# Order of the work at chunk borders in a hybrid decoder step: one product chain prioritised, one split cut in two, one weight cast queued later

## The chip, the cores and the metric

One core of a Trainium2 chip runs the whole program. The metric is the device time of one execution in microseconds, as the median of the timed runs. PE is the matrix engine (PEld its weight loads), DVE the vector engine, ACT the scalar engine, POOL the GpSimd engine, SP the engine that only issues DMAs here. Each engine takes its instructions in the order in which they were put into its queue.

## The reference

One inference step of a decoder trunk, in fp32, on 520 tokens (512 of a prompt, 8 of samples): a SwiGLU feed-forward network (FFN), a mixer (causal pooling beside a state-space scan), a second FFN, a final norm.

```python
def _swiglu(x, wg, wu, wd):
    return (jax.nn.silu(x @ wg) * (x @ wu)) @ wd

h = h + 0.5 * _swiglu(_rms_norm(h, ffn1_norm[l]), ffn1_w_gate[l], ffn1_w_up[l], ffn1_w_down[l])
m, p, c, s = _hybrid_mixer(_rms_norm(h, mix_norm[l]), ...)
h = h + m
h = h + 0.5 * _swiglu(_rms_norm(h, ffn2_norm[l]), ffn2_w_gate[l], ffn2_w_up[l], ffn2_w_down[l])
```

The model width is 1024, the hidden width of each FFN 2816, that is 22 tiles of 128. The change touches the two FFNs alone.

## The kernel before

**Precision.** An fp32 product is made of three passes of a faster fp32r product (`mm3`, lines 123, 126, 127): each operand is split into a high part (an ACT cast, line 107 for weights, 268 for activations) and a low part (the difference, a DVE subtraction, lines 114 and 269). For some halves of the weights the low part is made in another way: ACT writes the negated operand (line 110), and a DMA from the POOL queue adds the original weight onto it from memory (line 111).

**Seven products for eight.** The 520 tokens are two halves of 260. A *step* multiplies a 2x2 block of weights with a 2x2 block of activations (two row groups by two halves of tokens) in seven products instead of eight. For that, sums and differences of weight blocks and of activation blocks are formed. For the activations they stand in seven *slots* of 260 columns: slots 0 to 2 are plain blocks, slots 3 to 6 are differences. The products are numbered 1 to 7, and product 1 reads slot 0, 2 reads 1, 3 reads 2, 7 reads 4, 5 reads 3, 6 reads 5, 4 reads 6. In a step they are traced in the order 1, then product 4 of the step before, then 5, 6, 3, 7, 2 (`step`, `product`, `flush`). The results gather in PSUM tiles A and BE. ACT copies partial results out of them to `ac` (line 437); a later product that adds onto the same tile has to wait for that copy.

**Weights of a step.** `load` takes two raw tiles (one buffer `raw`, two of them in turn, loaded by two SP DMAs, line 366), adds them up on DVE (lines 385 to 387) and splits four groups: `a` (products 1 and 2), `c` (products 7 and 5), `d` (products 6 and 3), `b` (product 4). The names in the profile end in these letters: whi_1d_0b is the high part of group b of FFN 1, a down step, chunk 0 (buffer and row numbers are left out). Groups a and b have three buffers together (whi, wlo), c and d two (shi, slo). The last reader of a raw buffer is group b's negated copy.

**Chunks.** The 22 hidden tiles are taken in chunks of 6, 6, 6 and 4. For the first three (`PAIRED`), the gate/up steps (profile names by number, whi_5a) make the hidden activations, and then four down steps multiply them with the down weights (profile names A1d, BE1d, A2d, BE2d for PSUM, digit 1 or 2 for the FFN). Between the last gate/up step of a chunk and its first down step, the first gate/up step of the next chunk is put, so that PE has work while the last hidden tile is finished. The fourth chunk goes another way (`down`, `down_by_half`).

**The chain at a border.** When the products of a hidden tile are done, `gates` runs: DVE adds the copies (line 449), multiplies by the norm's scale (455), ACT applies Silu (456), DVE multiplies again (458) and then with the up part (`up`, 464; half of the tokens here, the other half in `close`, once product 4 is done). For the second tile of each pair `g_split` then forms the slots: DVE makes three differences (272, 273, 274) into `gd`, and `low` casts and subtracts (268, 269) slot 0 (gx), slot 2 and slots 3 to 5 (one instruction of 780 columns); with the second half, a fourth difference (282) and slots 1 and 6. For the last tile of a chunk this is done in two parts in this way; for the others all at once.

**What sets the order.** The program is traced once; a planner with a model of the engines' times then puts each engine's instructions in an order, from what it holds to be ready and from priorities. `tc.high_priority()` raises the priority of what is traced inside it; `tc.issue_after(ins)` puts what is traced inside it, on the engine of `ins`, behind `ins` in that engine's queue, without waiting for its end. In the second FFN each step also carries a small part of the state update of the mixer (`state`), whose ACT and POOL work is kept in its own order.

Of the kernel before, what the change touches and what calls it, by code (L numbers as in the profile page):

```python
# [11 lines left out]
AF = mybir.ActivationFunctionType  # L12
ALU = mybir.AluOpType
# [8 lines left out]
HB = NT // 2  # L22
# [12 lines left out]
PAIRED = 3  # L35
# [26 lines left out]
def tile_trunk_step(ctx: ExitStack, tc: tile.TileContext, ins: dict, outs: dict):  # L62
    nc = tc.nc
# [6 lines left out]
    wp = ctx.enter_context(tc.tile_pool(name="wp", bufs=3, side="right"))  # L70
# [9 lines left out]
    h = vx[:, NVEC:].rearrange("p (d t) -> p d t", d=KD)  # L80
# [10 lines left out]
        hp, nb = (wp, 2) if hp is None else (hp, 1)  # L91
        return hp.tile([P, 2, 1024], F32, tag="raw", bufs=nb, name=f"raw_{name}")

    half = []

    def raw_tile(name):
        if not half:
# [4 lines left out]
    def split(src, n, name, hp, nb, tags, late=None):  # L102
        hi, lo = (hp.tile([P, 1024], F32R, tag=t, bufs=nb, name=f"{t}_{name}")[:, :n] for t in tags)
        h, l = hi, lo
        if len(src.shape) == 3:
            h, l = (t.rearrange("p (j c) -> p j c", j=src.shape[1]) for t in (hi, lo))
        nc.scalar.copy(h, src)  # L107
        q = 0 if late is None else n - late.shape[1]
        if late is not None:
            nc.scalar.activation(out=lo[:, q:], in_=src[:, q:], func=AF.Copy, scale=-1.0)  # L110
            nc.gpsimd.dma_start(out=lo[:, q:], in_=late, accum_op=ALU.add)
        if late is None or q:
            s = slice(0, q) if late is not None else slice(None)
            nc.vector.tensor_tensor(out=l[:, s], in0=src[:, s], in1=h[:, s].bitcast(F32), op=ALU.subtract)
        return hi, lo

    def load_unit(src, n, name, late=False):
        raw = raw_tile(name)[:, :n]
        nc.sync.dma_start(out=raw, in_=src)
        return split(raw, n, name, wp, 3, ("whi", "wlo"), src if late else None)  # L120
# [87 lines left out]
    class Ffn:  # L208
# [42 lines left out]
        def g_split(self, f, late=None):  # L251
            role = self.role(f)
            if role == "plain" and late is not False:
                self.g_plain(f, self.out[f])
            if role != "second":
                return
            last = f == self.chunks[self.chunk[f]][-1]
            if not last and late is False:
                return
            gx, go = self.gx, self.out[f]  # L260
            if not last or late is not True:
                self.gt[f] = (self.gp.tile([P, 14, HB], F32R, tag="gt", bufs=3, name=f"gt{self.i}_{f}"),
                              self.gp.tile([P, 4, HB], F32, tag="xd", name=f"gd{self.i}_{f}"))
            t, xd = self.gt[f]

            def low(x, q):
                hi, lo = t[:, 0:7][:, q], t[:, 7:14][:, q]
                nc.scalar.copy(hi, x)
                nc.vector.tensor_tensor(out=lo, in0=x, in1=hi.bitcast(F32), op=ALU.subtract)

            if not last or late is not True:
                nc.vector.tensor_tensor(out=xd[:, 0], in0=gx[:, 0], in1=gx[:, 1], op=ALU.subtract)
                nc.vector.tensor_tensor(out=xd[:, 1], in0=go[:, 1], in1=gx[:, 1], op=ALU.subtract)
                nc.vector.scalar_tensor_tensor(out=xd[:, 2], in0=xd[:, 1], scalar=-1.0, in1=gx[:, 0], op0=ALU.mult,
                                               op1=ALU.subtract)
                low(gx[:, 0], 0)
                if last:
                    low(go[:, 1], 2)
                    low(xd[:, 0:3], slice(3, 6))
            if last and late is False:  # L280
                return
            nc.vector.scalar_tensor_tensor(out=xd[:, 3], in0=xd[:, 2], scalar=-1.0, in1=go[:, 0], op0=ALU.mult,
                                           op1=ALU.subtract)
            if last:
                low(go[:, 0], 1)
                low(xd[:, 3], 6)
            else:
                low(go, slice(1, 3))
                low(xd, slice(3, 7))
# [101 lines left out]
        def load(self, k):  # L391
            wx = self.wx
            n, src, nb, raw, f1, f2, add = self.added.pop(k) if k in self.added else self.sums(k)
            d1 = split(raw[:, 0, : 2 * nb], 2 * nb, f"{n}a", wp, 3, ("whi", "wlo"), src[0, :, nb:])
            if add is not None:
                add()
            e1 = split(f1, 2 * nb, f"{n}c", wx, 2, ("shi", "slo"))
            e2 = split(f2, 2 * nb, f"{n}d", wx, 2, ("shi", "slo"))
            d2 = split(raw[:, 1, nb : 2 * nb], nb, f"{n}b", wp, 3, ("whi", "wlo"), src[1, :, nb:])
            m = nb // P  # L400
            self.w[k] = {1: (d1, 0), 2: (d1, m), 7: (e1, 0), 5: (e1, m), 6: (e2, 0), 3: (e2, m), 4: (d2, 0)}

# [41 lines left out]
        def gates(self, k):  # L444
            n = f"{self.i}_{k}" if not isinstance(k, tuple) else f"{self.i}d{k[1]}_{k[0]}"
            r = self.nx[3].rearrange("p (b t) -> p b t", b=2)
            tg = self.tg[k] = self.wx.tile([P, 2, HB], F32, tag="tg", bufs=2, name=f"tg{n}")
            a, c = self.ac[k]
            nc.vector.tensor_tensor(out=tg, in0=self.BE[k][:, :, :HB], in1=a, op=ALU.add)  # L449
            if isinstance(k, tuple):  # L450
                hd, hn = h[:, k[1]], h[:, k[1] + 1, HALVES[1]]
                nc.vector.tensor_tensor(out=hd, in0=hd, in1=tg.rearrange("p b t -> p (b t)"), op=ALU.add)
                nc.vector.tensor_tensor(out=hn, in0=hn, in1=c[:, 0], op=ALU.subtract)
                return
            nc.vector.tensor_tensor(out=tg, in0=tg, in1=r, op=ALU.mult)  # L455
            nc.scalar.activation(out=tg, in_=tg, func=AF.Silu)  # L456
            self.g_homes(k)
            nc.vector.tensor_tensor(out=tg, in0=tg, in1=r, op=ALU.mult)  # L458
            self.up(k, 1, c[:, 0])
            self.g_split(k, False)  # L460

        def up(self, k, b, u):
            out, tg = self.out[k][:, b], self.tg[k][:, b]
# [2 lines left out]
        def close(self, k):  # L466
            if isinstance(k, tuple):
                hn = h[:, k[1] + 1, HALVES[0]]
                nc.vector.tensor_tensor(out=hn, in0=hn, in1=self.A[k][:, :HB], op=ALU.subtract)
                return  # L470
            self.up(k, 0, self.A[k][:, :HB])
            self.g_split(k, True)

        def scales(self):
            return rstds(self.nx, f"f{self.i}")
# [823 lines left out]
```

## Time and profile before

| | |
|---|---|
| timed runs | 973.34, 981.19, 981.55 us; median 981.19 us |
| profiled execution | 977.54 us, of which the span from first to last instruction is 975.8 us |
| granted PE clock of the profiled execution | 0.995 |
| instructions on PE, DVE, ACT, POOL | 7636, 1610, 1287, 341 |
| first FFN | to about 357 us of the span |
| mixer | about 357 to 624 us |
| second FFN | from about 602 us to the end |

How to read the rows: an instruction's row gives its start in us from the span's start, its length, the engine, the line of the kernel, the operation, what it writes and reads, the shape, and how many were merged into the row; in square brackets the idle time of its engine before it, and whose end ended that idle time. Rows of groups give busy time, mean ns of one, and idle time before. PE's matmuls overlap each other: one shows 0.28 us, and in a dense stretch the next starts 0.12 us after it. SPq is the queue of SP, in which the loads are issued.

### The profile page before, as it was taken

The page shows a single profiled execution, that of the slowest core. Times are in us where ns is not written, and L with a number is a line of the kernel's source. Part 1 is how long each engine was busy: PE and PEld are TensorE (multiplying, and loading weights), DVE is VectorE, ACT ScalarE, POOL GpSimd, SP SyncE. Part 2 cuts the span into 40 slices and gives each one's busy share as a digit, 9 for nine tenths or more (in the row PEclk, how much of TensorE's full clock was granted, in tenths as well). Part 3 has the DMA queues.
Part 4 walks back from the last instruction along what each step waited for, and adds up shares of the span by engine and source line. Part 5 has one row for each costly group of instructions (what it writes and reads, how often), then busy time and mean ns, then how long its engine had stood idle before and what let it go on. Part 6 is the DMA issues. An engine that isn't in the chain of part 4 may idle for free.

```text
span 975.8 us, 20309 instructions
## 1 busy us (share of the span) xinstructions
PE 945.4 (97%) x7636; PEld 924.0 (95%) x7636; DVE 856.6 (88%) x1610; ACT 700.3 (72%) x1287; POOL 233.6 (24%) x341
## 2 busy tenths in 40 slices
PE   7999999999999999999899999999999999999995
PEld 6999999999999999999799999899999999999995
DVE  7999899989989698688879866999989999999876
ACT  8776777777777475686676546678778788887864
POOL 0111211221121000156522111122332333333300
PEclk9999999999999999999999999999999999999998
DMA  7665766576566243264588777467687678777732
GB/s 242 167 154 136 190 149 148 126 184 180 119 152 165 66 150 118 88 205 117 148 232 225 177 173 165 119 146 179 152 220 185 167 174 222 178 159 189 191 90 89
DMA packets 66739, 157.01 MB, mean 161 GB/s; under 512 B 9608, under 2 KB 22856, under 8 KB 66640
## 3 DMA queue, kind: packets, MB, share of 16 engines
q1 hardware_dynamic: 41168, 103.78, 33.5%
q0 software_dynamic: 25472, 51.92, 29.3%
q8 instruction: 60, 0.98, 0.4%
q14 instruction: 39, 0.32, 0.1%
HBM read 148.33 MB, written 7.34 MB: 160 GB/s over the span
## 4 chain that ended last, share of the span: by engine, by line
PE 81%; DVE 7%; ACT 4%; DMA 4%; issue 2%; POOL 1%; SPq 0%; DVEq 0%; ACTq 0%; POOLq 0%
PE A L127 7%; PE A L123 7%; PE A L126 7%; PE BE L123 6%; PE BE L126 6%; PE BE L127 6%; PE P L315 3%; PE wo L123 2%; PE wo L127 2%; PE wo L126 2%; PE A1d L127 2%; PE A1d L126 2%; PE A1d L123 2%; DMA ab<-scr_acs 1%; PE A2d L127 1%
## 5 line engine op out<-in xcount | busy, mean ns | idle before, releaser
L437 ACT COPY ac<-A 128x260 f32<-128x260 f32 x123 | 45.3, 370 | 20.5 <-PE A L127 20.1
L385 DVE TENSOR_TENSOR s<-raw 128x1024 f32<-128x1024 f32 x41 | 49.9, 1217 | 2.6 <-DMA raw<-in_w2gu 2.4
L1005 POOL DMA_DIRECT2D out_nss<-hs x32 | 20.6, 643 | 84.3 <-DVE hs L1023 74.9
L123 PE MATMUL inz<-xh_mx,whi_inz 128*128 128x260 f32 x128 | 37.5, 293 | 1.0 <-DVE E L1099 1.0
L315 PE MATMUL P<-xg_f,raw 128*128 128x260 f32 x128 | 32.7, 409 | 5.4 <-DMA raw<-in_w1gu 5.4
L123 PE MATMUL wo<-catg,whi_wo 128*128 128x260 f32 x128 | 37.1, 290 | 0.0
L126 PE MATMUL inz<-xl_mx,whi_inz 128*128 128x260 f32 x128 | 36.9, 288 | 0.0
L127 PE MATMUL inz<-xh_mx,wlo_inz 128*128 128x260 f32 x128 | 36.9, 288 | 0.0
L123 PE MATMUL inx<-xh_mx,whi_inx 128*128 128x260 f32 x128 | 36.4, 285 | 0.0
L127 PE MATMUL wo<-catg,wlo_wo 128*128 128x260 f32 x128 | 36.2, 283 | 0.0
L127 PE MATMUL inx<-xh_mx,wlo_inx 128*128 128x260 f32 x128 | 36.2, 283 | 0.0
L126 PE MATMUL wo<-catg,whi_wo 128*128 128x260 f32 x128 | 36.1, 282 | 0.0
L126 PE MATMUL inx<-xl_mx,whi_inx 128*128 128x260 f32 x128 | 36.1, 282 | 0.0
L315 PEld LDWEIGHTS P<-xg_f,raw 128*128 128x128 f32 x128 | 25.7, 205 | 9.5 <-ACT xg_f L192 5.4
L449 DVE TENSOR_TENSOR tg<-BE,ac 128x520 f32<-128x520 f32 x41 | 28.4, 692 | 5.2 <-PE BE L127 5.2
L869 DVE SCALAR_TENSOR_TENSOR A<-U,h,A 128x544 f32<-128x544 f32 x36 | 28.1, 781 | 4.9 <-ACT A L867 4.6
L107 ACT CAST whi_wo<-raw_wo 128x1024 fp32r<-128x1024 f32 x12 | 12.6, 1047 | 27.0 <-issue 18.1
L1123 DVE TENSOR_TENSOR h<-wo,h 128x260 f32<-128x260 f32 x48 | 19.4, 419 | 13.7 <-PE wo L127 13.7
L458 DVE TENSOR_TENSOR tg<-tg,r_f 128x520 f32<-128x520 f32 x41 | 28.4, 693 | 1.2 <-ACT tg L456 1.0
L975 DVE SCALAR_TENSOR_TENSOR junk<-h,cb 128x128 f32<-128x128 f32 x64 | 21.5, 335 | 8.2 <-DMA cb<-scr_bc 7.3
L455 DVE TENSOR_TENSOR tg<-tg,r_f 128x520 f32<-128x520 f32 x41 | 28.4, 692 | 0.1
L386 DVE TENSOR_TENSOR s<-s,raw 128x512 f32<-128x512 f32 x41 | 28.0, 682 | 0.0
(1802 smaller groups left out, 4805.6 us busy)
## 6 DMA issues: line engine op xcount, KB each, us to landing
raw<-in_w2gu SPq DMA_DIRECT2D x44, 512.0 KB, 5.0
raw<-in_w1gu SPq DMA_DIRECT2D x42, 512.0 KB, 4.6
raw_1d<-in_w1d SPq DMA_DIRECT2D x24, 384.0 KB, 3.9
raw_2d<-in_w2d SPq DMA_DIRECT2D x24, 384.0 KB, 4.1
raw_wo<-in_w_out SPq DMA_DIRECT2D x12, 512.0 KB, 6.1
wlo_wo<-in_w_out POOLq DMA_DIRECT2D x12, 512.0 KB, 7.4
ab<-scr_acs SPq DMA_DIRECT2D x8, 512.0 KB, 5.4
h<-in_state_ssm SPq DMA_DIRECT2D x16, 256.0 KB, 6.5
```

The source lines that it names most:

```text
L123: first = nc.tensor.matmul(ps, whi, xhi, start=start, stop=False, **kw)
L126: nc.tensor.matmul(ps, whi, xlo, start=False, stop=False, **kw)
L127: nc.tensor.matmul(ps, wlo, xhi, start=False, stop=stop, **kw)
L315: nc.tensor.matmul(self.banks[f, u][b][:, :HB], ws(self.raw[f][:, u], j + 4 * q), xg[:, slot[q]], start=j == q == 0, stop=j == 3 and q == ...
L385: nc.vector.tensor_tensor(out=s1, in0=diag, in1=up0, op=ALU.add)
L386: nc.vector.tensor_tensor(out=s2[:, 0], in0=s1[:, 1], in1=raw[:, 0, :nb], op=ALU.add)
L437: nc.scalar.copy(keep, out[:, :HB])
L449: nc.vector.tensor_tensor(out=tg, in0=self.BE[k][:, :, :HB], in1=a, op=ALU.add)
L455: nc.vector.tensor_tensor(out=tg, in0=tg, in1=r, op=ALU.mult)
L458: nc.vector.tensor_tensor(out=tg, in0=tg, in1=r, op=ALU.mult)
L869: nc.vector.scalar_tensor_tensor(out=A[:, :n], in0=U[:, j : j + n], scalar=w(j), in1=A[:, :n], op0=ALU.mult, op1=ALU.add)
L975: nc.vector.scalar_tensor_tensor(out=junk, in0=h0[:, q], scalar=1.0, in1=cb, op0=ALU.mult, op1=ALU.mult, accum_out=ysm[:, 4 * g + q, b : b ...
```

## The change

Three things are changed, all in the FFNs.

1. `g_split`: the third difference is computed from the first instead of from the second (the same value), and for the last tile of a chunk slot 3 is split alone, then slots 4 and 5 together, then slot 2; before, slot 2 was split first and then slots 3 to 5 together.
2. `load`: every ACT cast of a weight split is noted, and group b's split (cast and negated copy on ACT) is queued behind the newest one, which is group d's cast. This holds for gate/up and for down steps.
3. `first_if`: for the last tile of each of the three paired chunks, the multiplications, the Silu, the up part and the forming of the slots are traced with high priority, both in `gates` and in `close`.

```diff
-        nc.scalar.copy(h, src)
+        cast = nc.scalar.copy(h, src)
+        casts.append(cast.ins)
...
-                nc.vector.scalar_tensor_tensor(out=xd[:, 2], in0=xd[:, 1], scalar=-1.0, in1=gx[:, 0], op0=ALU.mult,
+                nc.vector.scalar_tensor_tensor(out=xd[:, 2], in0=xd[:, 0], scalar=-1.0, in1=go[:, 1], op0=ALU.mult,
                                                op1=ALU.subtract)
                 low(gx[:, 0], 0)
                 if last:
+                    low(xd[:, 0], 3)
+                    low(xd[:, 1:3], slice(4, 6))
                     low(go[:, 1], 2)
-                    low(xd[:, 0:3], slice(3, 6))
...
             e2 = split(f2, 2 * nb, f"{n}d", wx, 2, ("shi", "slo"))
-            d2 = split(raw[:, 1, nb : 2 * nb], nb, f"{n}b", wp, 3, ("whi", "wlo"), src[1, :, nb:])
+            with tc.issue_after(casts[-1]):
+                d2 = split(raw[:, 1, nb : 2 * nb], nb, f"{n}b", wp, 3, ("whi", "wlo"), src[1, :, nb:])
...
-            nc.vector.tensor_tensor(out=tg, in0=tg, in1=r, op=ALU.mult)
-            nc.scalar.activation(out=tg, in_=tg, func=AF.Silu)
-            self.g_homes(k)
-            nc.vector.tensor_tensor(out=tg, in0=tg, in1=r, op=ALU.mult)
-            self.up(k, 1, c[:, 0])
-            self.g_split(k, False)
+            with self.first_if(k):
+                nc.vector.tensor_tensor(out=tg, in0=tg, in1=r, op=ALU.mult)
+                nc.scalar.activation(out=tg, in_=tg, func=AF.Silu)
+                self.g_homes(k)
+                nc.vector.tensor_tensor(out=tg, in0=tg, in1=r, op=ALU.mult)
+                self.up(k, 1, c[:, 0])
+                self.g_split(k, False)
+
+        def first_if(self, k):
+            c = self.chunk[k]
+            return tc.high_priority() if c < PAIRED and k == self.chunks[c][-1] else nullcontext()
...
-            self.up(k, 0, self.A[k][:, :HB])
-            self.g_split(k, True)
+            with self.first_if(k):
+                self.up(k, 0, self.A[k][:, :HB])
+                self.g_split(k, True)
```

More of the change, by code (lines that the diff above doesn't have):

```diff
@@ L92, in raw_pair @@
         return hp.tile([P, 2, 1024], F32, tag="raw", bufs=nb, name=f"raw_{name}")
-    half = []
+    half, casts = [], []
     def raw_tile(name):
```

## The prediction

> **What bounds the kernel now.** I read the page first, for the share of each engine, then the list of waits of PE over the two stretches with chunk borders, then the order of time at one border, engine by engine. The page says that PE is the bound:
>
> ```profile
> PE 945.4 (97%) x7636; PEld 924.0 (95%) x7636; DVE 856.6 (88%) x1610; ACT 700.3 (72%) x1287; POOL 233.6 (24%) x341
> ```
>
> A change to DVE and ACT can therefore win only what PE stands still for. PE's waits from 60 to 300 us (first FFN, chunks with borders), and from 690 to 900 us (second FFN); the columns are total idle, times, longest:
>
> ```profile
> core 0 of [0], span 975.8 us
> engine line waited for: us in total, times, longest us
> PE BE1d L126 <- DVE gt L269: 0.9, 3, 0.3
> PE BE1d L123 <- ACT ac1d L437: 0.8, 3, 0.3
> ```
>
> ```profile
> PE BE2d L126 <- DVE gt L269: 1.7, 2, 0.8
> PE BE2d L123 <- ACT ac2d L437: 1.3, 3, 0.7
> PE A2d L127 <- DVE slo_2d_0d L114: 0.7, 1, 0.7
> ```
>
> These are the six borders: the first down step of a chunk waits for the low half of the last product's differences (L269), and right after for an evacuation copy (L437). Eleven stops, 4.7 us of idle; the twelfth (slo_2d_0d) is a weight's low half. Idle is not all that a stop costs, as PE's order of time at the first border shows:
>
> ```profile
> 89.38 0.28 PE L123 MATMUL A1d<-gt,shi_1d_0d 128*128 128x260 f32 x1
> 89.95 0.39 PE L126 MATMUL BE1d<-gt,shi_1d_0c 128*128 128x260 f32 x1 [0.29 <-DVE gt L269]
> 90.18 0.28 PE L127 MATMUL BE1d<-gt,slo_1d_0c 128*128 128x260 f32 x1
> 90.30 0.28 PE L126 MATMUL A1d<-gt,shi_1d_0d 128*128 128x260 f32 x1
> 90.42 0.28 PE L127 MATMUL A1d<-gt,slo_1d_0d 128*128 128x260 f32 x1
> 90.98 0.39 PE L123 MATMUL BE1d<-gt,shi_1d_0d 128*128 128x260 f32 x1 [0.28 <-ACT ac1d L437]
> 91.21 0.29 PE L126 MATMUL BE1d<-gt,shi_1d_0d 128*128 128x260 f32 x1
> ```
>
> Starts are 0.12 us apart when nothing is missing (90.18, 90.30, 90.42). Here they are 0.57, 0.23, 0.56 and 0.23 apart at the two stops, so 0.45+0.11+0.44+0.11 = 1.11 us are lost where the idle column shows 0.57: each stop costs 0.27 us above its idle. Eleven stops cost 4.7 + 11 x 0.27 = 7.7 us, the twelfth 0.7 + 0.27 = 1.0 us. That 7.7 is the most that the border edits can win, 0.8% of the span.
>
> **The change, part by part.** First the priority on the last product of a chunk (`first_if`). ACT and DVE at the same border:
>
> ```profile
> 78.33 0.38 ACT L437 COPY ac<-BE 128x260 f32<-128x260 f32 x1 [0.87 <-DVE ac L439]
> 79.61 0.83 ACT L107 CAST whi_1d_0a<-raw_1d 128x768 fp32r<-128x768 f32 x1 [0.90 <-PE A L126]
> 80.35 0.52 ACT L110 ACTIVATE wlo_1d_0a<-raw_1d 128x384 fp32r<-128x384 f32 x1
> 80.77 0.62 ACT L456 ACTIVATE tg<-tg 128x520 f32<-128x520 f32 x1
> ...
> 86.36 0.85 ACT L268 CAST gt<-gd 128x780 fp32r<-128x780 f32 x1
> ```
>
> ```profile
> 78.25 0.69 DVE L455 TENSOR_TENSOR tg<-tg,r_f 128x520 f32<-128x520 f32 x1
> ...
> 80.47 0.56 DVE L114 TENSOR_TENSOR wlo_1d_0a<-raw_1d,whi_1d_0a 128x384 fp32r<-128x384 f32 x1 [1.06 <-ACT whi_1d_0a L107]
> 80.95 0.55 DVE L387 TENSOR_TENSOR s_1d<-s_1d,raw_1d 128x384 f32<-128x384 f32 x1
> 81.43 0.70 DVE L458 TENSOR_TENSOR tg<-tg,r_f 128x520 f32<-128x520 f32 x1
> ...
> 84.63 0.42 DVE L274 SCALAR_TENSOR_TENSOR gd<-gd,gx 128x260 f32<-128x260 f32 x1
> ...
> 88.94 1.30 DVE L269 TENSOR_TENSOR gt<-gd,gt 128x780 fp32r<-128x780 f32 x2
> ```
>
> The Silu's input was done at 78.94 (78.25 + 0.69), the Silu ran at 80.77: 1.83 us behind a weight cast that itself stood 0.90 us until PE gave its buffer free. The differences were done at 85.05 (84.63 + 0.42), their cast started at 86.36 (1.3 us), was done at 87.21, and the low half started at 88.94 (1.7 us). So 4.8 us of this chain is queueing behind other work, against a lateness of 0.57 us here and 0.8 + 0.27 = 1.1 us in the second FFN. The Silu (0.62) fits in the 0.90 us in which ACT stood still and the multiplication after it (0.70) in the 1.06 us in which DVE did, so overtaking there costs the overtaken weight cast nothing. Without that cover it would set the cast back by 0.62 us.
>
> When the low half comes in time, what is late next? The copy of product 5, for which product 3 waits. It was late only because product 5 ended behind most of product 6. In order, product 6 stands between them: nine matmuls, 9 x 0.12 = 1.1 us, over a copy of 0.38 us. So both stops of a border go together.
>
> The third difference from the first instead of the second is one instruction of the same shape in the same place (L274, 0.42 us): 0. It only lets it go before the second is done.
>
> The split alone. Slot 3 is what product 5 needs; it now comes before slots 4 and 5 and before slot 2, which is the order of need (5, 6, 3). It adds one ACT and one DVE instruction at each of six borders. DVE by form:
>
> ```profile
> L269 DVE TENSOR_TENSOR gt<-tg,gt 128x520 fp32r<-128x520 f32 x12 | 8.3, 694 | 1.1 <-ACT gt L268 1.0
> ...
> L269 DVE TENSOR_TENSOR gt<-gd,gt 128x780 fp32r<-128x780 f32 x6 | 5.8, 959 | 0.0
> ```
>
> One of 780 (0.96) becomes one of 520 (0.69) and one of 260 (0.42, as L274): 0.15 us more, 0.9 us for six; on ACT at most one more 260 (0.38), 2.3 us for six. At zero on the path, hidden in the DVE idle of 1.06 us; 0.9 us if that is gone. In return the first low half needs a cast and a subtraction a third as wide: 0.85 - 0.38 = 0.47 and 0.96 - 0.42 = 0.54 us sooner, 1.0 us, nearly the whole lateness even if the priority moved nothing. The Trainium skill (Perfetto Trace Analysis, Optimizing Scalar/DVE Operations) speaks against it for a full engine: it says to group into larger operations when the engine is saturated, at about 60 ns a DVE and 93 ns a ScalarE instruction, and to break up only where an unsaturated engine makes another stand idle. By its figures an estimate is 0.36 us DVE and 0.56 us ACT for six; with DVE at 88% I follow its second half, and the sum stays.
>
> Last, the weight cast for product 4 behind the one for products 6 and 3 (`issue_after`). This is no border edit: it holds in all 65 loads (41 gate/up, 24 down), and it adds a wait in ACT's queue. An ordinary down step now:
>
> ```profile
> 101.34 0.52 ACT L110 ACTIVATE wlo_1d_0b<-raw_1d 128x384 fp32r<-128x384 f32 x1
> 102.23 0.83 ACT L107 CAST shi_1d_0d<-s_1d 128x768 fp32r<-128x768 f32 x1 [0.37 <-PE A1d L126]
> ```
>
> ```profile
> 101.89 0.33 SPq L366 DMA_DIRECT2D raw<-in_w1gu  x1
> ```
>
> The negated copy (L110, ends 101.86) is the last reader of the raw buffer, and SP issues the load after next 0.03 us later. Behind shi_1d_0d (to 103.06) the cast and the copy (0.52 each, as the row) end at 104.1 at the soonest: POOL's accumulating DMA and SP's load both go 2.2 us later, more where evacuation copies come between. Who waits: product 4, a step later, and L385 on DVE, the first reader of the next raw. What a late raw costs stands in one place of the trace:
>
> ```profile
> L385 DVE TENSOR_TENSOR s<-raw 128x1024 f32<-128x1024 f32 x41 | 49.9, 1217 | 2.6 <-DMA raw<-in_w2gu 2.4
> ```
>
> ```profile
> 716.45 1.22 DVE L385 TENSOR_TENSOR s<-raw 128x1024 f32<-128x1024 f32 x1 [1.90 <-DMA raw<-in_w2gu]
> 717.59 0.69 DVE L449 TENSOR_TENSOR tg2d<-BE2d,ac2d 128x520 f32<-128x520 f32 x1
> 718.20 0.95 DVE L114 TENSOR_TENSOR slo_2d_0d<-s_2d,shi_2d_0d 128x768 fp32r<-128x768 f32 x1
> ```
>
> L385 held DVE for 1.90 us at the end of the second FFN's first down stage, slo_2d_0d came late, and that is PE's twelfth stop: 1.0 us for a late load. In the other 40 loads of this kind only 0.7 us were lost, so most have something in hand. Below, the price of the step is 0 and not a gain: shi_1d_0d stood 0.37 us for PE itself, so taking work from ahead of it does not start it sooner. Above, it is 1.0 us in each of the 24 down loads. I take the nearest row: that the same place at the second FFN's other two down stages also falls late, 2 x 1.0.
>
> Sum against the profiled execution (span 975.8, 977.5 with what lies around it): -7.7 + 2.0 = -5.7, 971.8 us. The three timed runs are 973.3, 981.2 and 981.6; the profiled one lies 3.7 below their median, so against the median 981.2 - 5.7 = **975.5 us**.
>
> **The rivals.** (A) The next wait takes over. With PE 1.1 us earlier at a border it may wait for that step's later weights, whose casts wait for buffers that PE frees; or ACT's copies stand behind the moved casts (0.52) for as much as was won. For it: ACT's casts at the border wait on PE in the rows above. Against: 4.8 us of queueing against 1.1. No change: 981.
>
> That the priority does not do what it says is a part of the forecast: ACT was free at 78.71 (78.33 + 0.38), the Silu's input done only at 78.94, so a planner that takes what is ready takes the cast first, whatever the priority. The split is left then, 1.0 of 1.1 us a border: about -6 + 2 = -4, 977.
>
> (B) More than the borders goes: the twelfth stop too, and no new late load: -7.7 - 1.0 = -8.7. On the median that is 972.5, on the fastest run 964.6; about 969 between them, which the spread of runs (8.2 us) can carry past 1%. For it: the moved cast also leaves ACT's queue ahead of the twelfth stop. Against: that stop came from a load.
>
> (C) Slower: the raw loads. 2.2 us later is more than the down steps have in hand, DVE stands at L385 in each of the 24, PE stops 1.0 us each time: 24 - 7.7 = +16.3, 997.5. It decides from 8 stops (even); over 1% slower from 18. For it: the one place above. Against: it is one of 41, and if the planner knows of the later landing it puts L385 later. The Trainium skill (DMA: Bandwidth & Descriptors, Issuing engines are not separate DMA queues) says that SP's and GpSimd's transfers run on the same 16 DMA engines and interleave; by that the moved load also slows the moved accumulate, which makes (C) likelier. No row here prices it.
>
> **How the numbers follow.** About 1% (9.8 us) is what three runs of this kernel can tell from no change. Forecast 0.50 (its own range 969 to 981), (A) 0.25, (B) 0.13, (C) 0.12. Low end: the fastest run less all of 7.7, 965.6, so 966. High end: the slowest run, 981.6, plus three late loads and some, 985; (C) is left out. Faster by over 1% comes from (B) and a little of the forecast, 0.14; slower from (C), 0.12; the rest 0.74.
>
> **What would show it.** Right: no PE wait on gt L269 in the down steps, the Silu L456 of a chunk's last product right behind L455, two L268 casts of 260 and 520 where one of 780 was, at a border. The load step: L110 of the b weight behind the d cast, SP's load 2 to 4 us later, L385 with more idle on DMA. Wrong: new PE waits on L114, L437 or the b weights all along the down steps, or border stops as before.

## The result, and the profile after

| | before | after |
|---|---|---|
| timed runs, median (lowest to highest) | 979.74 us (973.34 to 981.55, 6 runs) | 989.79 us (984.85 to 995.49, 6 runs) |
| ratio after/before, 95% interval | | 1.012 (1.0084 to 1.0155) |
| a second series, beside the first experiments | 979.26 us (29 runs) | 987.16 us (12 runs), 1.0088 (1.0059 to 1.0117) |
| span of the profiled execution | 975.8 us | 989.3 us |

The change makes the kernel about 1% slower. The prediction had 975.5 us, a range of 966 to 985 us, and 12% for slower.

Lines of this program lie 1 to 9 further down than before: L269 of before is L270, L385 is L387, L437 is L440, L114 is L115, L110 is L111 (in the experiments a few lines further still). The first line of the page, then PE's waits from 60 to 300 us (first FFN) and from 640 to 950 us (second FFN), columns as in the prediction:

```profile
PE 951.5 (96%) x7636; PEld 926.0 (94%) x7636; DVE 858.0 (87%) x1616; ACT 687.8 (70%) x1293; POOL 233.3 (24%) x341
```

```profile
PE A1d L128 <- DVE slo_1d_1d L115: 0.2, 1, 0.2
```

```profile
PE A2d L124 <- ACT ac2d L440: 3.0, 9, 0.4
PE A L128 <- DVE slo_7d L115: 1.4, 1, 1.4
PE BE L124 <- ACT ac L440: 1.1, 1, 1.1
PE A L124 <- ACT ac L440: 1.0, 3, 0.4
PE A L128 <- DVE slo_1d L115: 0.9, 1, 0.9
PE BE2d L124 <- ACT shi_2d_1c L107: 0.9, 1, 0.9
PE BE2d L124 <- ACT shi_2d_2c L107: 0.9, 1, 0.9
PE A2d L128 <- DVE slo_2d_1d L115: 0.7, 1, 0.7
PE A2d L128 <- DMA wlo_2d_1b<-in_w2d: 0.3, 1, 0.3
PE A L128 <- DVE slo_10d L115: 0.2, 1, 0.2
```

(Over 640 to 950 us, the kernel before has one stop besides those that the prediction shows for its shorter stretch: 0.3 us for the copy ac.) The border stops of before are gone in both FFNs: no wait on gt is left. The first FFN has one stop of 0.2 us where it had six. The second has new ones all along: nine times a down step waits for an evacuation copy, four low halves come late from DVE and one from its accumulating DMA, and twice product 5's weight cast is late.

Where the time went is read from PE's starts: the first FFN from the first matmul of its step 1 to the mixer's first matmul, the mixer to the first matmul of step 3 of the second FFN (plain fp32 products of the second FFN start some 15 us sooner, among the mixer's), the second FFN to the first matmul of the final norm.

| us | first FFN | mixer | second FFN |
|---|---|---|---|
| before | 321.7 | 253.1 | 348.1 |
| after | 319.3 | 258.3 | 358.7 |
| after, second profile | 319.3 | 254.2 | 360.0 |

The first FFN won 2.4 us (2.7 where it is counted from the span's start, as the expectations below do), the second lost 10.6 and 11.9. The stage times are from single profiles; the 16 profiles of kernels with all three parts in the first FFN have 318.9 to 320.3 us there, so differences of about 1 us between two profiles say little. The mixer, whose instructions stand in the same order on every engine in both programs, was 5.2 us longer in one profile and 1.1 in the other; that is taken up in the last section. Gain and loss of the two FFNs, 8.2 and 9.5 us, are 0.8 to 1.0%; that is the ratio of the second series (0.9%) and the lower end of the first one's interval (1.2%, 0.8 to 1.6%).

What the loss of the second FFN is made of can be added up from the intervals between PE's starts: each above 0.2 us or with a wait, less the 0.12 us of a dense stretch, put down to what ended the wait. This is a count by attribution: freed of one wait, PE may meet another. The sum is 14.5 us before and 25.3 after, 10.8 more, as the stage says.

| us in the second FFN | before | after |
|---|---|---|
| low halves of the activations (gt) | 2.0 | 0 |
| product 5's weight cast at a border (shi c) | 0 | 2.0 |
| evacuation copies (ac, ac2d) | 5.3 | 10.0 |
| weights' low halves from DVE (slo) | 1.1 | 3.9 |
| weights' low halves from accumulating DMAs (wlo) | 0 | 0.5 |
| last down weights, and late starts without a wait of their own | 6.1 | 8.9 |

### The profile page after: what moved, and what is told of

Its sections match the earlier page's. It is cut to its first block, busy times and chain, and to the rows that moved or that the text cites. A ratio compares the mean times of both kernels' runs of the same rounds, so it can differ in the third digit from the quotient of the medians.

```text
span 989.3 us, 20228 instructions
## 1 busy us (share of the span) xinstructions
PE 951.5 (96%) x7636; PEld 926.0 (94%) x7636; DVE 858.0 (87%) x1616; ACT 687.8 (70%) x1293; POOL 233.3 (24%) x341
## 4 chain that ended last, share of the span: by engine, by line
PE 41%; DMA 5%; ACT 4%; DVE 4%; issue 2%; POOL 1%; SPq 0%; DVEq 0%; ACTq 0%; POOLq 0%
PE A L124 4%; PE A L128 4%; PE A L127 3%; PE BE L124 3%; PE BE L127 3%; PE BE L128 3%; PE wo L124 2%; PE wo L128 2%; PE wo L127 2%; DMA raw<-in_w2gu 2%; DMA ab<-scr_acs 1%; PE A2d L124 1%; DMA cb<-scr_bc 1%; PE A2d L128 1%; PE A2d L127 1%
## 5 line engine op out<-in xcount | busy, mean ns | idle before, releaser
L387 DVE TENSOR_TENSOR s<-raw 128x1024 f32<-128x1024 f32 x41 | 49.9, 1217 | 10.7 <-DMA raw<-in_w2gu 6.4
L440 ACT COPY ac<-A 128x260 f32<-128x260 f32 x123 | 45.2, 368 | 15.7 <-PE A L128 15.6
L984 DVE SCALAR_TENSOR_TENSOR junk<-h,cb 128x128 f32<-128x128 f32 x64 | 21.7, 340 | 12.6 <-DMA cb<-scr_bc 11.7
L460 ACT ACTIVATE tg<-tg 128x520 f32<-128x520 f32 x41 | 26.2, 639 | 4.8 <-DVE tg L459 4.7
```

The lines of the kernel that those rows point to most:

```text
L387: nc.vector.tensor_tensor(out=s1, in0=diag, in1=up0, op=ALU.add)
L440: nc.scalar.copy(keep, out[:, :HB])
```

## The experiments

**Which part loses: each half of the change alone.** Every ratio is to runs of the kernel before on the same chip. Undone in the first kernel is only the order of the cast; the second has only that order; the third has it in the first FFN only; the fourth is the changed kernel again.

```diff
 e1
-            with tc.issue_after(casts[-1]):
+            with nullcontext():
 e2 (g_split as before, and)
-            return tc.high_priority() if c < PAIRED and k == self.chunks[c][-1] else nullcontext()
+            return nullcontext()
 e3
-            with tc.issue_after(casts[-1]):
+            with tc.issue_after(casts[-1]) if self.i == 1 else nullcontext():
```

> The whole change except the order of the weight cast for product 4 (border edits alone). Theory L (the later cast makes the raw loads late in the second FFN, where DVE has little to spare): the second FFN no longer loses its 10.5 us, the first FFN keeps its 2.7 us or more: 5 to 8 us below the kernel before, ratio 0.992 to 0.995, if the mixer takes its time of before. Theory B (the priority at the borders pushes the second FFN's load work back): as slow as the changed kernel, ratio 1.01. Theory M (the 5.3 us lost in the mixer, whose queues are in the same order, come with any shift in time): 5 us less gain, ratio about 1.0.

> The kernel before with only the weight cast for product 4 put behind the fifth product's. Theory L: slower by what the changed kernel lost in the second FFN and what the borders won besides, ratio 1.012 to 1.02; DVE stands at the first addition of a raw load (s from raw, second FFN) for some 10 us where it was 2.6. Theory B: no change, ratio 1.0.

> The whole change, with the cast order in the first FFN only. Theory L: the first FFN gains the 2.7 us that the changed kernel showed there, the second gains at its borders, 5 to 8 us below before, as with the border edits alone; if the cast order itself helped the first FFN, 1 to 2 us below the run without it, if it cost there, above it. Theory B: ratio 1.01.

> The changed kernel once more, for a second profile. Theory L: second FFN some 10 us longer than before, in the same places. Theory M as chance of transfers: the mixer's loss of 5.3 us is not the same in this profile; as a fixed consequence of the shift: it is there again, within 1 us.

| | ratio to before (95%) | first FFN | mixer | second FFN |
|---|---|---|---|---|
| e1, border edits alone | 1.0034 (1.0002 to 1.0066) | 323.5 | 254.4 | 348.4 |
| e2, cast order alone | 1.0152 (1.0109 to 1.0196) | 323.0 | 252.5 | 359.6 |
| e3, cast order in the first FFN only | 0.9986 (0.9957 to 1.0016) | 320.0 | 254.0 | 349.4 |
| e0, the changed kernel again | 1.0088 (1.0059 to 1.0117) | 319.3 | 254.2 | 360.0 |

The loss is the cast order, in the second FFN: 11.5 us without the border edits (359.6 - 348.1), 9.3 to 10.6 with them (358.7 and 360.0 against e3's 349.4). The theory that the priority pushes load work back falls: e1 is not as slow as the changed kernel. But the 5 to 8 us that were expected of e1 and e3 did not come either. In the first FFN the border edits alone cost 1.8 us and the cast order alone 1.3; only both together win 2.4. (The 1.3 us, from one profile, is little more than the spread.) PE's waits in the first FFN of e1 say why:

```profile
PE BE1d L124 <- ACT shi_1d_2c L107: 1.4, 1, 1.4
PE BE1d L124 <- ACT shi_1d_0c L107: 1.4, 1, 1.4
PE BE1d L124 <- ACT shi_1d_1c L107: 1.4, 1, 1.4
```

ACT and PE there, in order of time:

```profile
91.38 0.51 ACT L107 CAST whi_1d_0b<-raw_1d 128x384 fp32r<-128x384 f32 x1 [1.22 <-PE BE1d L127]
91.80 0.52 ACT L111 ACTIVATE wlo_1d_0b<-raw_1d 128x384 fp32r<-128x384 f32 x1
92.22 0.81 ACT L107 CAST shi_1d_0c<-s_1d 128x768 fp32r<-128x768 f32 x1
```

```profile
93.09 0.39 PE L124 MATMUL BE1d<-gt,shi_1d_0c 128*128 128x260 f32 x1 [1.39 <-ACT shi_1d_0c L107]
```

With the border's chain moved up, ACT came early to the second down step. The next instruction in its queue was the cast for product 4, which PE needs last; it stood 1.22 us until PE had read out its buffer, and the cast for product 5, which PE needs first, stood behind it. So the two stops of a border, 0.57 us idle together, became one longer stop of 1.39, which is rival (A) of the prediction, and the cast order is what removes it: it takes product 4's cast out of that place. It is a border edit after all.

**Where the cast order may stay in the second FFN.** e4 has it there in the second down step of each chunk only, e5 in all down steps, e13 in the gate/up loads only; e7 puts the cast behind that for products 7 and 5, one cast earlier.

```diff
 e4
+            with tc.issue_after(casts[-1]) if self.i == 1 or k in ((0, 2), (1, 2), (2, 2)) else nullcontext():
 e5
+            with tc.issue_after(casts[-1]) if self.i == 1 or isinstance(k, tuple) else nullcontext():
 e13
+            with tc.issue_after(casts[-1]) if self.i == 1 or not isinstance(k, tuple) else nullcontext():
 e7
+            with tc.issue_after(casts[-1 if self.i == 1 else -2]):
```

> The whole change, with the cast order in all loads of the first FFN, but in the second FFN only in the load of each chunk's second down step (3 of 32). Theory: the border edits need the cast order at this one load (without it product 5 of the second down step waits 1.4 us for a cast that stands behind the weight cast of product 4), and everywhere else in the second FFN it only makes loads late. Then the second FFN wins its borders: 3 x 1.7 us below the run with the order in the first FFN only, 969 to 972 us, ratio 0.990 to 0.994. If the moved cast costs at single loads too: no better than that run, ratio 0.998.

> The whole change, with the cast order in the first FFN and in the down steps of the second FFN, not in its gate/up loads. If the loss comes from the gate/up loads (whose transfers are the larger ones): ratio 0.990 to 0.996. If it comes from the down loads: as slow as the changed kernel, 1.008 to 1.012. If from both: between them.

> The whole change, with the cast order in the first FFN and in the gate/up loads of the second FFN, not in its down loads. Theory of two causes (late raw buffers in the gate/up loads, evacuation copies behind the moved cast in the down steps, about 5 us each): the second FFN loses some 5 us more than with the cast order in the first FFN only, ratio 1.003 to 1.006; PE's waits for the copy ac2d are gone, DVE's idle at the first addition from raw stays at 6 us or more in the second FFN. If one cause were the whole: 1.000 or 1.009.

> The whole change, with the cast order as it is in the first FFN; in the second FFN the weight cast for product 4 is put behind the cast for products 7 and 5 only, one cast earlier. Theory: this still removes the wait of the second down step's product 5, and the raw buffers come free earlier by a cast: ratio 0.990 to 0.996. If any delay of the cast costs there: between the run with the order in the first FFN only and the changed kernel, 1.000 to 1.008.

| | ratio to before (95%) | first FFN | mixer | second FFN |
|---|---|---|---|---|
| e4, second down steps | 1.0008 (0.9982 to 1.0034) | 319.0 | 253.0 | 350.6 |
| e5, all down steps | 1.0068 (1.0034 to 1.0102) | 318.9 | 251.9 | 354.4 |
| e13, gate/up loads | 1.002 (0.9989 to 1.005) | 319.2 | 256.4 | 351.6 |
| e7, one cast earlier | 1.0 (0.9977 to 1.0024) | 319.6 | 253.1 | 348.2 |

Both kinds of load cost: against e3 (349.4) the down loads 5.0 us and the gate/up loads 2.2, where 5 each was expected; the timed ratio of e13 does not exclude that the latter cost nothing. In e13, PE's waits for ac2d are gone, as expected, but DVE stood 4.2 us for raw loads of the second FFN and not 6. Together both kinds cost 9.3 to 10.6, so some 2 to 3 us would come only when both are late; single profiles do not make that firm. One cast earlier costs nothing (e7). None wins what e4 was to win.

How a down load costs is seen on ACT and PE in e5:

```profile
791.63 0.51 ACT L107 CAST whi_2d_1b<-raw_2d 128x384 fp32r<-128x384 f32 x1
792.04 0.37 ACT L440 COPY ac2d<-A2d 128x260 f32<-128x260 f32 x1
792.31 0.40 ACT L1030 ACTIVATE hs<-hs,sdec 128x128 f32<-128x128 f32 x1
...
793.20 0.39 ACT L1031 ACTIVATE so<-br,sxdt 128x128 f32<-128x128 f32 x1
793.50 0.51 ACT L111 ACTIVATE wlo_2d_1b<-raw_2d 128x384 fp32r<-128x384 f32 x1
793.91 0.35 ACT L440 COPY ac2d<-A2d 128x260 f32<-128x260 f32 x1
```

```profile
794.32 0.39 PE L124 MATMUL A2d<-gt,shi_2d_1d 128*128 128x260 f32 x1 [0.34 <-ACT ac2d L440]
```

The cast takes the place behind group d's, and its negated copy (793.50) goes behind the four small pieces of state update that the second FFN carries, and so right ahead of product 1's evacuation copy (793.91), for which product 6 waits. That is the row of nine stops of the changed kernel.

How a gate/up load costs is seen in the changed kernel, on ACT, SP, DVE and PE:

```profile
726.75 1.05 ACT L107 CAST shi_9d<-s 128x1024 fp32r<-128x1024 f32 x1 [1.33 <-PE A2d L127]
727.70 0.62 ACT L107 CAST whi_9b<-raw 128x512 fp32r<-128x512 f32 x1
...
729.68 0.62 ACT L111 ACTIVATE wlo_9b<-raw 128x512 fp32r<-128x512 f32 x1
...
730.32 1.19 SPq L368 DMA_DIRECT2D raw<-in_w2gu  x2
...
739.58 1.23 DVE L387 TENSOR_TENSOR s<-raw 128x1024 f32<-128x1024 f32 x1 [2.99 <-DMA raw<-in_w2gu]
741.33 1.22 DVE L115 TENSOR_TENSOR slo_7d<-s,shi_7d 128x1024 fp32r<-128x1024 f32 x1
...
742.60 0.39 PE L128 MATMUL A<-xth_f,slo_7d 128*128 128x260 f32 x1 [1.41 <-DVE slo_7d L115]
```

The same step before:

```profile
722.90 0.63 ACT L110 ACTIVATE wlo_9b<-raw 128x512 fp32r<-128x512 f32 x1
723.46 1.05 ACT L107 CAST shi_9d<-s 128x1024 fp32r<-128x1024 f32 x1
...
723.56 0.88 SPq L366 DMA_DIRECT2D raw<-in_w2gu  x2
...
733.16 1.21 DVE L385 TENSOR_TENSOR s<-raw 128x1024 f32<-128x1024 f32 x1
```

Before, the negated copy ended 0.07 us behind the start of group d's cast (723.53 and 723.46), and SP issued the next raw load but one at 723.56; DVE used it 9.6 us later without a wait. By the trace the second of its two transfers, issued at 723.93, landed at 732.81, so this load had some 0.3 us in hand. After, it ended 3.55 us behind that start (730.30 and 726.75), the load was issued at 730.32, and DVE stood 2.99 us for it though it started 9.26 us after the issue. The load takes as long as it did, 8.8 us from the second issue to landing against 8.9; it starts late. (It is the slowest of its kind in both traces, whose medians are 4.7 and 5.0 us.) The low half slo_7d stood behind it on DVE, and PE behind that.

**Is it the late buffer?** e6 leaves product 4's cast and its transfer where they were in the second FFN, and lets ACT read 8 columns of the raw buffer right behind product 1's copy, so that the buffer alone comes free late. e14 is its control, with the same small read directly behind product 4's cast.

```diff
 e6 (cast order in the first FFN only, and)
+            self.last_read = raw[:, 1, 2 * nb - 8 : 2 * nb]
...
-                nc.scalar.copy(keep, out[:, :HB])
+                cp = nc.scalar.copy(keep, out[:, :HB])
+                if p == 1 and self.i == 2:
+                    with tc.issue_after(cp.ins):
+                        nc.scalar.copy(self.wx.tile([P, 8], F32, tag="tch", bufs=1, name=f"tch_{self.i}_{k}"), self.last_read)
 e14 (cast order in the first FFN only, and)
+            if self.i == 2:
+                with tc.issue_after(casts[-1]):
+                    nc.scalar.copy(wx.tile([P, 8], F32, tag="tch", bufs=1, name=f"tch_{n}"), raw[:, 1, 2 * nb - 8 : 2 * nb])
```

> The cast order in the first FFN only, and in the second FFN one more reader of each raw buffer: ACT copies 8 columns of it right behind product 1's copy of the step, the place where the negated copy stands in the changed kernel; the weight cast of product 4 and its accumulating transfer stay early. Theory late raw (the raw buffer comes free late, so the next load but one lands late and DVE stands at its first addition): slower by most of what the changed kernel lost in its second FFN, 5 to 10 us above the run with the order in the first FFN only, idle of DVE at the first addition from raw 6 us or more in the second FFN. Theory ACT order or late low half (what costs is product 4's weight itself, or copies behind it): no more than the 35 small copies, within 2 us of that run.

> Control for the late reader: the same copy of 8 columns of each raw buffer in the second FFN, but directly behind the weight cast of product 4 and ahead of its negated copy, so that the raw buffer comes free as early as ever. Theory late raw: as fast as the run with the cast order in the first FFN only, ratio 0.998 to 1.001, DVE's idle at the first addition from raw under 4 us in the second FFN. If the small copies themselves cost: 1.003 to 1.006, as with the late reader.

e6: ratio 1.0043 (1.0016 to 1.0069), second FFN 354.2 us. e14: 1.0005 (0.9978 to 1.0032), 350.0 us. The group of the first addition, in e6 and then in e14:

```profile
L387 DVE TENSOR_TENSOR s<-raw 128x1024 f32<-128x1024 f32 x41 | 50.0, 1220 | 10.8 <-DMA raw<-in_w2gu 6.4 <-DMA raw<-in_w1gu 2.3 <-issue 1.9
```

```profile
L387 DVE TENSOR_TENSOR s<-raw 128x1024 f32<-128x1024 f32 x41 | 50.0, 1218 | 5.9 <-DMA raw<-in_w2gu 3.7 <-DMA raw<-in_w1gu 2.2
```

PE's waits for weights' low halves in e6's second FFN; of the four, e14 has the first alone, with 1.4 us:

```profile
PE A2d L128 <- DVE slo_2d_1d L115: 1.6, 1, 1.6
...
PE A2d L128 <- DVE slo_2d_2d L115: 1.4, 1, 1.4
PE A L128 <- DVE slo_10d L115: 0.7, 1, 0.7
PE A2d L128 <- DVE slo_2d_0d L115: 0.7, 1, 0.7
```

The late buffer alone costs 4.2 us (354.2 - 350.0), with no weight moved; the timed ratios, 1.0043 and 1.0005, are 3.7 us apart. This is less than the 5 to 10 us that were expected. It does not bring the waits for copies. So the loss has more than one cause, and the late buffer by itself makes some two fifths of it.

**Is the rest the copies?** e11 is e5 with the negated copy behind product 1's evacuation copy, a swap of two neighbours.

```diff
 e11 (e5, with the negated copy and its transfer put into self.deferred in the second FFN's down loads, and)
-                nc.scalar.copy(keep, out[:, :HB])
+                cp = nc.scalar.copy(keep, out[:, :HB])
+                if p == 1 and self.deferred:
+                    with tc.issue_after(cp.ins):
+                        self.deferred.pop()()
```

> As the run with the cast order in the down steps of the second FFN, but the negated copy of product 4's weight stands behind product 1's evacuation copy on ACT instead of ahead of it: one swap of two neighbours in each of 12 down steps. Theory: half of the loss in the second FFN comes from PE's product 6 waiting for that evacuation copy (0.3 us idle and 0.25 to restart, nine to eleven times); these stops go, 4 to 6 us below the run without the swap, ratio about 1.001. If the late raw buffers cost there: no gain, since the raw buffer comes free 0.3 us later still, ratio 1.006 to 1.008.

1.0039 (1.0011 to 1.0068), second FFN 353.7 us, where e5 had 1.0068 and 354.4: 0.7 us in the profile, not the 4 to 6 of the expectation. The eight waits A2d <- ac2d of e5 (2.8 us) are gone, and in their place is one for the other thing that hangs on the same instruction, the accumulated low half:

```profile
PE A2d L133 <- DMA wlo_2d_2b<-in_w2d: 1.7, 1, 1.7
```

By the count of intervals used above, the copies cost 4.0 us less in e11 than in e5 (5.0 against 9.0), and the accumulated low halves 2.0 more (2.3 against 0.3). So the copies are shown to wait for the moved cast, but how much of the loss they make is not settled: freed of one, the step waits for the next.

**Why the border edits win nothing in the second FFN.** e8 has the whole change in the first FFN only, e9 has in addition the new difference and the split alone in the second (no priority, no cast order). e10 is e7 with product 5 of the second down step held in its place in PE's order, e12 also product 3 of the first down step, e15 also splits slots 5 and 4 one by one.

```diff
 e8, e9
-            with tc.issue_after(casts[-1]):
+            with tc.issue_after(casts[-1]) if self.i == 1 else nullcontext():
...
-            return tc.high_priority() if c < PAIRED and k == self.chunks[c][-1] else nullcontext()
+            return tc.high_priority() if self.i == 1 and c < PAIRED and k == self.chunks[c][-1] else nullcontext()
 e8 alone
+                nc.vector.scalar_tensor_tensor(out=xd[:, 2], in0=xd[:, 0 if self.i == 1 else 1], scalar=-1.0, in1=go[:, 1] if self.i == 1 else gx[:, 0], op0=ALU.mult,
...
-                if last:
+                if last and self.i == 1:
                     low(xd[:, 0], 3)
                     low(xd[:, 1:3], slice(4, 6))
                     low(go[:, 1], 2)
+                elif last:
+                    low(go[:, 1], 2)
+                    low(xd[:, 0:3], slice(3, 6))
 e10 (on top of e7; e12 has (p, k[1]) in ((5, 2), (3, 0)))
-                    j == n - 1, skip_group_check=True)
+                    j == n - 1, pin=p == 5 and j == 0 and self.i == 2 and isinstance(k, tuple) and k[1] == 2,
+                    skip_group_check=True)
 e15 (on top of e12)
-                    low(xd[:, 1:3], slice(4, 6))
+                    low(xd[:, 2], 5)
                     low(go[:, 1], 2)
+                    low(xd[:, 1], 4)
```

> All three parts of the change in the first FFN only; the second FFN as in the kernel before. Theory: the first FFN keeps the 2 to 3.5 us that the five runs with all three parts showed there, the second and the mixer are as before: ratio 0.996 to 0.998. If the whole change gained nothing even there, 1.000.

> As the run with the change in the first FFN only, and in the second FFN the third difference from the first and slot 3 split alone, without priority and without the cast order. Theory: the split alone brings the low half 1.0 us sooner, which takes most of the 0.85 us stops and what hangs on them: 2 to 4 us below the run with the change in the first FFN only, ratio 0.993 to 0.996. If the priority was what moved the chain: no difference from that run.

> As the run with the product 4 cast behind products 7 and 5's in the second FFN, and product 5 of each second down step held to its place in the program's order on PE (behind product 7 and 2 of the first step and products 1 and 4). There PE stood 0.9 and 0.2 us at each of three borders because the planner had put two matmuls of product 5 ahead of product 7 of the step before, while their weight's buffer was still being read. Theory: these stops go, 3 x (0.9 + 0.2 + 0.5) = some 4 to 5 us below that run, 970 us or less, ratio 0.990 to 0.996. If only the stop moves on to the next product: no difference from that run, 1.000.

> As the run with product 5 of the second down step held in place, and product 3 of each chunk's first down step held behind product 6 as well (second FFN). In that run PE stood 1.5 us at each border, since the planner had put the last two matmuls of product 6 behind products 3 and 2, and product 6's evacuation copy then stood on ACT behind two weight casts. Theory: with both held, the copy is ahead of the casts, all stops of the second FFN's borders but a few tenths go: 4 to 6 us below that run, ratio 0.993 to 0.996. If a wait for the low halves takes its place: ratio 0.998 to 1.000.

> The run with two products held in place once more, for a narrower interval of the version that came out ahead of both kernels in its first run (0.998, 0.9947 to 1.0012). Its stages without the mixer were 3.9 us below before; if that is the gain, ratio 0.994 to 0.998; if the first run was chance, 1.000.

> As that version, with slots 5 and 4 split one by one in the order of need (3, 5, 2, 4) instead of together. There PE still stood 0.4 us at each border of the second FFN for the low half of slots 4 and 5. Theory: that stop goes, 1 to 1.8 us below the version with slots 4 and 5 together, for 0.15 us more of DVE at each border. If DVE has no room for the added instruction: no difference or up to 1 us above.

| | ratio to before (95%) | first FFN | mixer | second FFN |
|---|---|---|---|---|
| e8, first FFN only | 0.999 (0.9965 to 1.0015) | 319.2 | 250.9 | 347.0 |
| e9, and the split in the second | 0.9999 (0.9974 to 1.0023) | 320.3 | 254.0 | 348.8 |
| e10, product 5 held | 0.9989 (0.9958 to 1.002) | 320.1 | 258.5 | 349.4 |
| e12, product 3 held too | 0.998 (0.9947 to 1.0012) | 319.3 | 254.7 | 346.9 |
| e12 again | 0.9993 (0.9963 to 1.0022) | 319.8 | 258.6 | 347.3 |
| e15, slots one by one | 0.9997 (0.9966 to 1.0027) | 319.1 | 258.3 | 347.7 |

Up to e12 each removed the stop at which it was aimed, and each time the next one was there; e15 did not remove its own, three waits on gt of up to 0.5 us. PE's waits in the second FFN of e9, e10 and e12, in this order:

```profile
PE BE2d L124 <- ACT shi_2d_0c L107: 1.4, 1, 1.4
PE BE2d L124 <- ACT shi_2d_1c L107: 1.4, 1, 1.4
PE BE2d L124 <- ACT shi_2d_2c L107: 1.4, 1, 1.4
```

```profile
PE A2d L124 <- ACT ac2d L441: 4.6, 3, 1.5
```

```profile
PE A2d L127 <- DVE gt L270: 1.3, 3, 0.4
```

e9 shows that the split alone is enough to be rid of the waits on gt, and that the stop for the cast of product 5 takes their place, as in e1; e3, which has the priority there as well, took 349.4 us against 348.8, so no gain of the priority is shown. e10 traded that for product 6's copy. e12 has the shortest second FFN of the runs with border edits, 346.9 and 347.3; but e8, whose second FFN is that of before, took 347.0 in its profile. The border edits win nothing there that these profiles can tell. No version was shown to be faster than the kernel before: e3, e8, e10 and e12 lie 0.1 to 0.2% below it, with intervals that reach above 1. The 2.4 us of the first FFN, 0.25%, are less than these intervals can tell.

## Why the prediction was wrong, step by step

**The bound** was read rightly: PE, and all that was won or lost was won or lost in PE's stops.

**The border edits, "7.7".** In the changed kernel the first FFN won 2.4 us, of 3 x 1.11 = 3.3 that the prediction had there. That it came so near is luck: the border edits alone lost 1.8 there (e1), and what turned this into a gain is the cast order, which the prediction entered as a price. In the second FFN the stops on gt went, and PE then stood for product 5's weight cast; e1 and e9 show the same wait, and e10 and e12 the next one each time it is removed. This is rival (A), at 0.25. Its mark against, 4.8 us of queueing against 1.1 of lateness, counted only the chain of the activations; the second step's weights have a chain of their own.

**The split alone, "1.0 us sooner"**, was right in direction and mis-sized. ACT and DVE of the changed kernel at the first border:

```profile
77.22 0.40 ACT L269 CAST gt<-gd 128x260 fp32r<-128x260 f32 x1
78.28 0.64 ACT L460 ACTIVATE tg<-tg 128x520 f32<-128x520 f32 x1
...
83.52 0.62 ACT L269 CAST gt<-gd 128x520 fp32r<-128x520 f32 x1
```

```profile
76.45 0.69 DVE L459 TENSOR_TENSOR tg<-tg,r_f 128x520 f32<-128x520 f32 x1
...
78.54 0.42 DVE L270 TENSOR_TENSOR gt<-gd,gt 128x260 fp32r<-128x260 f32 x1
```

Slot 3 is the difference of the two halves of the pair's first tile alone; it needs nothing of the last tile. In one instruction with slots 4 and 5 it had to wait for them; alone, it was cast at 77.22, ahead of the last tile's Silu (78.28), and its low half was done at 78.96. Before, that low half began at 88.94. The prediction counted the shorter instructions and not what each slot depends on. The Silu came 1.1 us behind its input (77.14 to 78.28), where it was 1.83; the two casts of 260 and 520 are where one of 780 was. These marks of "what would show it" came true.

**"This is no border edit"**, said of the weight cast, is wrong, as e1 and e2 show: in the first FFN the border edits need it to win anything.

**The delay, "2.2 us later"**, was right for the first FFN, whose rows it came from, and little more than half of what it is in the second. Over all steps, from product 1's first matmul to the end of the negated copy, the median shift is 2.3 us (down loads) and 2.5 (gate/up loads) in the first FFN, and 3.5 and 4.1 in the second, where four pieces of state update and evacuation copies stand between.

**The price, "2 x 1.0"**, is the step that failed: 9.3 to 11.5 us in place of 2.0. Two things went wrong in it. It asked who waits for the moved instructions (product 4, the raw load) and not who stands behind them in ACT's queue; product 1's copy does, and the prediction named such copies only in rival (A). And it took 0.7 us of waiting in 40 loads as a sign that they had something in hand. The row of 739.58 above shows a load that was used without a wait before and so was counted among the safe ones; it had some 0.3 us in hand, and a wait of zero says nothing of the margin.

Rival (C) had the mechanism of the late buffer, at 0.12, and put it into the 24 down loads of both FFNs at 1.0 us each; the runs show that it costs PE in the second FFN, gate/up loads included, 4.2 us together (e6 against e14), while the changed kernel's first FFN won time with the same loads late. It also cites the Trainium skill (DMA: Bandwidth & Descriptors, Issuing engines are not separate DMA queues) for SP's and GpSimd's transfers running on the same 16 DMA engines and interleaving. That did not make this load late: the load of 730.32 was not slower than its counterpart of before, it was issued later, and the two transfers started together before the change as well (what that costs is in the last section).

How much of the 9.3 to 11.5 us is the copies, and how much comes of the two causes together, stays open. Of the sum, -2.4 in the first FFN and +10.6 to 11.9 in the second stand where -7.7 + 2.0 was predicted.

## What to carry to other kernels

When an instruction is queued later, list three kinds of waiters: those for its result, those for the buffer that it frees, and those that stand behind it in its own queue; price each in the stage with the least slack, here the second FFN with its added state work. A wait of zero in the profile is not a margin: look at the landing time beside the first use. And where two edits are made together, ask which stop the first one uncovers and whether the second is there to cover it: they can each cost alone and win together.

## What the runs showed of the hardware

**Two transfers that start together.** Before, one instruction, the negated copy, releases both group b's accumulating transfer on the POOL queue and the next raw load on the SP queue. e6 parts the two in the second FFN: the raw load goes later, the transfer as early as ever. The transfer's median time from issue to landing is 6.3 us (down) and 6.0 (gate/up) in e14, where they are issued 0.1 us apart, and 3.9 and 4.2 in e6, where the load goes some 3 us later; the raw down loads took 4.1 us in e14 and 3.3 in e6. In the changed kernel the two are still issued 0.1 us apart, and group b's transfers take 6.0 and 6.2; what got slower there are group a's in the second FFN, from 3.9 and 4.0 us to 5.6 and 5.8, though none of PE's waits of the changed kernel shown above names one of those.

**The mixer's spread.** In all these kernels the mixer's instructions stand in the same order on PE, DVE, ACT and POOL as before, yet its time runs from 249.8 to 258.6 us over the 19 profiles. The difference shows in the waits for its transfers, above all that of DVE for the broadcast rows read back from memory. Before, e11 (the shortest) and e12 again (the longest), in this order:

```profile
DVE junk L975 <- DMA cb<-scr_bc: 7.3, 4, 3.8
```

```profile
DVE junk L994 <- DMA cb<-scr_bc: 7.8, 3, 4.5
```

```profile
DVE junk L985 <- DMA cb<-scr_bc: 14.7, 5, 6.9
```

The wait is twice as long in the longest as in the others. Over all 19 profiles it is 7.2 to 13.3 us where the mixer took under 255 us, and 11.7 to 14.7 where it took over 256; so the two go together, but not profile by profile, and what makes the transfer late was not tried. The spread is as large as the effect under study, so a single profile's span says little here (e10's span was 981.2 us, e8's 970.5, with timed medians of 977.4 and 977.6): the stages that do not hold the mixer had to be compared.
